# A DiT layer up to LayerNorm 1: the order of five engines read from a written list, the first two features in one group, warm-up matmuls only ahead of the first product

## The chip, the cores and the metric

The kernel runs on one core of a Trainium2 chip. It issues work to five engines: TensorE (PE in the profile, with its weight loads as PEld), VectorE (DVE), ScalarE (ACT), GpSimd (POOL) and SyncE (SP, which issues nearly all of the loads from device memory). Each engine takes its instructions strictly in the order in which they were issued to it. The metric is the device time of one execution, in microseconds (us). Lower is better.

## The reference

One layer of a diffusion transformer over 256 latent tokens `x` and 256 context tokens `ctx` with 2048 features, all in float32. Up to the place that matters here it computes:

```python
sh1, sc1, g1, sh2, sc2, g2 = silu(c) @ w_ada + b_ada          # split in six; w_ada is 2048 x 12288
csh1, csc1, ...            = silu(c_ctx) @ w_ada + b_ada
qa, ka, va, qb, kb, vb     = modulate(x, sh1, sc1) @ w_in     # modulate(x, s, c) = x * (1 + c) + s
qac, kac, vac, ...         = modulate(ctx, csh1, csc1) @ w_in
heads = concat(window_sink_attention(qa, ...), global_attention(qb, ...))
x = layer_norm(ALPHA * x + g1 * (heads @ w_out), ln1_g, ln1_b)
x = layer_norm(ALPHA * x + g2 * swiglu(modulate(x, sh2, sc2), ...), ln2_g, ln2_b)
```

So no product with `w_in` can start before a shift and a scale exist for its feature. Each shift and scale is a sum over a whole column of `w_ada`, 2048 rows long.

## The kernel before

**Tiles.** A "feature" below is a block of 128 of the 2048 model features, 0 to 15. A block of `w_in` has 512 output columns, and there are six, b = 0 to 5; blocks 2 and 5 hold keys and values and have four rows of outputs (two of `x`, two of `ctx`), the others hold queries and have two rows. A product in full float32 is three matmuls of 128x512 (`mm3`, L334 to 337): the weights are split into a rounded part `hi` and a remainder `lo`, and the scaled input into `uh` and `ul`. ACT makes `hi` (the cast in `flow_weights`, L603), DVE makes `lo` (L606).

**Groups.** `GROUPS` cuts the features into (0), (1), (2, 3), (4 to 7) and (8 to 15). For each group `flow_inputs` and `flow_columns` make a chain: load its columns of `w_ada`, sum them on PE into four partial rows (L654), copy these to SBUF on ACT (`ada`, L683), select and add on PE (L688), add the bias on DVE (`shc`, L694, and `scc`, L696); then transpose the inputs on PE ("flip", L822), scale them on ACT (`uf`, L828), cast on ACT (`uh`, L835), remainder on DVE (`ul`, L838). For features 12 to 15 (`VECTOR_K`) the columns are summed on DVE instead (`csum`, L716 and L718), transposed and reduced on DVE (L742, L745) and folded by PE (L769). `flow_block` then issues the products of one block with the group's features into an `acc` bank of PSUM. After a group, the result of a block goes to SBUF: for the first group as a copy (L887 on ACT, L891 on DVE), for the following ones as an addition on DVE (L889, into `qacc` or `kvacc`). From group number `SEED_G` = 3 on, the old sum is copied into the bank first, and no addition is needed.

**What sets the order.** Up to LayerNorm 1 nothing is issued directly. The functions named `flow_...` and some others add steps to an object `Flow`: engine, estimated time, the function that issues the instructions, the steps it comes after, and the buffers it takes and gives back. At build time `Flow.run` (L235) plans the order of all steps of all engines with a list scheduler forward and backward, tries 1400 random variations in a replay with estimated times, and issues the best. What comes after LayerNorm 1's scalars is issued by code behind `F.run()`.

**Warm-ups.** Besides five matmuls at the very start (`EARLY_WARM`), `WARM` = 56 further matmuls of `ident` with itself, whose result nobody reads, are steps of the plan (L1343). They have the lowest rank, each follows the one before, and together they hold one `wk` bank of PSUM until the last.

**First loads.** The ACT queue loads the first 128 columns of `x` and `ctx` (L380, L381). SP loads feature 0's columns of `w_ada`: 1 MB for the scale, 2 x 0.5 MB for the shift, 128 columns wide (rows of 512 bytes). Feature 1 follows with 2 MB of its own.

```python
for i in range(WARM):
    warms.append(F.add("PE", 430 if i < COLD else 225, lambda i=i: warm_step(i), [warms[-1]],
                       [wps] if i == 0 else [], [wps], at=1e6))
```

Of the kernel before, what the change touches and what calls it, by code (L numbers as in the profile page):

```python
# [23 lines left out]
P = 128  # L24
D = 2048
# [15 lines left out]
GROUPS = ((0, 1), (1, 1), (2, 2), (4, 4), (8, 8))  # L41
# [6 lines left out]
WARM = 56  # L48
VECTOR_K = (12,)
EARLY_WARM = 5  # L50
COLD = 3
SEED = 4
# [13 lines left out]
SEED_G = 3  # L66
# [3 lines left out]
GET_NS = 1300  # L70

# [11 lines left out]
class Flow:  # L83

    ENGINES = ("SP", "PE", "ACT", "DVE", "POOL")
    SAME = {"SP": 0, "PE": 0, "ACT": 120, "DVE": 80, "POOL": 80}
    OTHER = {"SP": 2000, "PE": 270, "ACT": 180, "DVE": 160, "POOL": 150}  # L90
    AGAIN = 1300
    ROUNDS = 8
    TRIES = 1400
    DRAWS = 4
    LATE = {"SP": 1000.0, "ACT": 100.0, "DVE": 100.0}

    def __init__(self, room, begin):
        self.room, self.begin, self.steps, self.at = dict(room), begin, [], 0.0

    def add(self, eng, ns, fn, after=(), take=(), give=(), at=None, since=0.0):  # L100
        s = Step()
        s.since = since
        s.eng, s.ns, s.fn, s.take, s.give = eng, ns, fn, take, give
        s.after = [a if isinstance(a, tuple) else (a, 0) for a in after if a is not None]
        s.rank = (self.at if at is None else at, len(self.steps))
        for b in give:
            b.left += 1
        self.steps.append(s)
        return s

    def lag(self, a, b):
        return (self.SAME if a.eng == b.eng else self.OTHER)[a.eng]

    def forward(self):

        room, free, back, order, now = dict(self.room), dict(self.begin), [], [], 0.0
        later, ready = ({e: [] for e in self.ENGINES} for _ in range(2))
        left = {b: b.left for s in self.steps for b in s.give}
        for s in self.steps:
            s.next, s.left, s.when = [], len(s.after), s.since  # L120
        for s in self.steps:
            for a, early in s.after:
                a.next.append((s, early))
            if not s.left:
                heapq.heappush(later[s.eng], (s.when, s.rank, s))
        while len(order) < len(self.steps):
            while back and back[0][0] <= now:
                room[heapq.heappop(back)[1]] += 1
            moved = False
            for e in self.ENGINES:  # L130
                while later[e] and later[e][0][0] <= now:
                    heapq.heappush(ready[e], heapq.heappop(later[e])[1:])
                if free[e] > now:
                    continue
                for item in sorted(ready[e]):
                    s = item[1]
                    pools = [next((p for p in b.pools if room[p] > 0), None) for b in s.take]
                    if None in pools or any(room[p] < pools.count(p) for p in pools):
                        continue
                    ready[e].remove(item)  # L140
                    heapq.heapify(ready[e])
                    for b, p in zip(s.take, pools):
                        b.pool = p
                        room[p] -= 1
                    s.start, free[e] = now, now + s.ns
                    for b in s.give:
                        left[b] -= 1
                        if left[b] == 0:
                            lag = self.AGAIN if b.loaded else self.OTHER[e]
                            heapq.heappush(back, (free[e] + lag, b.pool))  # L150
                    for n, early in s.next:
                        n.left -= 1
                        n.when = max(n.when, free[e] - early + self.lag(s, n))
                        if n.left == 0:
                            heapq.heappush(later[n.eng], (n.when, n.rank, n))
                    order.append(s)
                    moved = True
                    break
            if not moved:
                times = [free[e] for e in self.ENGINES if free[e] > now and (ready[e] or later[e])]  # L160
                times += [later[e][0][0] for e in self.ENGINES if later[e] and later[e][0][0] > now]
                times += [back[0][0]] if back else []
                if not times:
                    return None, None
                now = min(times)
        return order, max(s.start + s.ns for s in self.steps)

    def backward(self, end):

        free = {e: end for e in self.ENGINES}  # L170
        later, ready = ({e: [] for e in self.ENGINES} for _ in range(2))
        left, by, start, now = {s: len(s.next) for s in self.steps}, {s: end for s in self.steps}, {}, end
        for s in self.steps:
            if not left[s]:
                heapq.heappush(later[s.eng], (-end, -(s.start + s.ns), s.rank, s))
        while len(start) < len(self.steps):
            moved = False
            for e in self.ENGINES:
                while later[e] and -later[e][0][0] >= now:
                    heapq.heappush(ready[e], heapq.heappop(later[e])[1:])  # L180
                if free[e] < now or not ready[e]:
                    continue
                s = heapq.heappop(ready[e])[-1]
                start[s] = free[e] = now - s.ns
                moved = True
                for a, early in s.after:
                    left[a] -= 1
                    by[a] = min(by[a], start[s] + early - self.lag(a, s))
                    if left[a] == 0:
                        heapq.heappush(later[a.eng], (-by[a], -(a.start + a.ns), a.rank, a))  # L190
            if not moved:
                times = [free[e] for e in self.ENGINES if free[e] < now and (ready[e] or later[e])]
                now = max(times + [-later[e][0][0] for e in self.ENGINES if later[e] and -later[e][0][0] < now])
        return start

    def replay(self, order, draw):

        free, rooms, end, late = dict(self.begin), {p: [0.0] * n for p, n in self.room.items()}, {}, {}
        left = {b: b.left for s in self.steps for b in s.give}
        for s, pools in order:  # L200
            t = max(free[s.eng], s.since, *(end[a] - early + self.lag(a, s) for a, early in s.after), 0.0)
            for b, p in zip(s.take, pools):
                t = max(t, heapq.heappop(rooms[p]))
                b.pool = p
# [1768 lines left out]
```

## Time and profile before

| | |
|---|---|
| three runs | 1124.49, 1124.76, 1125.29 us (median 1124.76) |
| span of the profiled execution | 1124.1 us (the three runs are 0.4 to 1.2 us above it) |
| instructions | 14152 |
| warm-up matmuls of the plan (L1343) | 56, from 8.7 to 129.4 us |
| first product with `w_in` (L335) | 16.42 us |
| fold of the last column sums (L769) | 147.97 us |
| four flips that follow LayerNorm 1's scalars (L1510) | 393.79 us |

The profiler records two matmul passes for each float32 matmul of `ident`, of the sums (L654) and of the flips: "x30" of L1343 are 15 warm-ups. A matmul row's time begins when its data start to flow and ends at the modelled end, so rows overlap; the distance from one start to the next is what a matmul takes of PE's time. In the views by stage each line has the stretch, then busy time and count of PE, PEld, DVE, ACT and POOL, the granted clock of PE (1.00 is full), the busy share of the DMA engines and GB/s.

### The profile page before, as it was taken

How to read it: one execution, taken by the hardware profiler on the slowest of the kernel's cores; microseconds unless marked ns; L12 is line 12 of the kernel's file. 1: busy time of each engine (PE TensorE's matmuls, PEld its weight loads, DVE VectorE, ACT ScalarE, POOL GpSimd, SP SyncE). 2: the span in 40 equal slices, each digit the busy share in tenths (PEclk: the TensorE clock that was granted, in tenths of full speed). 3: DMA queues.
4: the chain of work that ended last, by engine and by line, in shares of the span. 5: the costliest groups of instructions: out<-in, count | busy, mean ns of one | idle time of the engine just before them, and what ended most of it. 6: DMA issues, size and time to landing. Idle time of an engine off the chain costs nothing.

```text
span 1124.1 us, 14152 instructions
## 1 busy us (share of the span) xinstructions
PE 1103.7 (98%) x5241; PEld 893.4 (79%) x5241; DVE 905.7 (81%) x1097; ACT 603.6 (54%) x879; POOL 47.1 (4%) x86
## 2 busy tenths in 40 slices
PE   8999999999999999999999999999999999999995
PEld 7677788788888778888888888888888788888884
DVE  3758999999989988787756876887875899678886
ACT  3335584787684355544464555655554565345541
POOL 1000050101200011000000000000000000000000
PEclk9999999999999999999999999999999999999998
DMA  9999999697999879989858798998896576546651
GB/s 298 388 391 373 390 366 370 225 312 215 356 311 375 303 284 341 326 309 340 295 189 297 264 340 273 314 308 302 311 321 222 159 253 223 190 149 231 225 217 75
DMA packets 179452, 321.27 MB, mean 286 GB/s; under 512 B 8979, under 2 KB 51379, under 8 KB 177077
## 3 DMA queue, kind: packets, MB, share of 16 engines
q1 hardware_dynamic: 177350, 319.23, 81.1%
q10 hardware_dynamic: 1808, 1.11, 0.3%
q8 instruction: 41, 0.67, 0.2%
q14 instruction: 29, 0.24, 0.1%
q0 software_dynamic: 224, 0.02, 0.0%
HBM read 304.07 MB, written 16.25 MB: 285 GB/s over the span
## 4 chain that ended last, share of the span: by engine, by line
PE 94%; DVE 3%; DMA 2%; issue 0%; ACT 0%; DVEq 0%; ACTq 0%
PE acc L335 22%; PE acc L336 22%; PE acc L337 22%; PE wk L337 7%; PE wk L336 7%; PE wk L335 7%; PE wk L1130 2%; PE wk L654 2%; PE wk L1343 1%; DMA raw<-in_w_in_dram 1%; PE wk L822 1%; DMA raw<-in_w_ada_dram 1%; DMA adav<-in_b_ada_dram 1%; DVE adav L454 0%; DVE lo L332 0%
## 5 line engine op out<-in xcount | busy, mean ns | idle before, releaser
L326 DVE TENSOR_TENSOR lo<-raw,hi 128x1024 fp32r<-128x1024 f32 x232 | 280.5, 1221 | 126.4 <-ACT hi L325 124.7
L325 ACT CAST hi<-raw 128x1024 fp32r<-128x1024 f32 x232 | 243.3, 1055 | 241.3 <-PE acc L337 130.7
L337 PE MATMUL acc<-hi,u2l 128*128 128x512 f32 x448 | 174.6, 390 | 1.4 <-DVE u2l L1686 1.4
L336 PE MATMUL acc<-lo,u2h 128*128 128x512 f32 x448 | 174.9, 390 | 0.0
L335 PE MATMUL acc<-hi,u2h 128*128 128x512 f32 x448 | 174.7, 391 | 0.0
L603 ACT CAST hi<-raw 128x1024 fp32r<-128x1024 f32 (+1 forms) x86 | 87.5, 1031 | 92.0 <-DMA raw<-in_w_in_dram 40.1
L454 DVE SCALAR_TENSOR_TENSOR adav<-raw,cs,adav 128x1024 f32<-128x1024 f32 (+1 forms) x96 | 114.3, 1191 | 6.1 <-DMA raw<-in_w_ada_dram 2.5
L606 DVE TENSOR_TENSOR lo<-raw,hi 128x1024 fp32r<-128x1024 f32 (+1 forms) x86 | 101.8, 1197 | 21.5 <-ACT hi L603 21.5
L335 PE MATMUL acc<-hi,uh 128*128 128x512 f32 x256 | 103.5, 404 | 0.2 <-DVE qacc L889 0.2
L335 PE MATMUL acc<-hi,hTh 128*128 128x512 f32 x264 | 102.7, 389 | 0.6 <-ACT hi L331 0.6
L336 PE MATMUL acc<-lo,hTh 128*128 128x512 f32 x264 | 102.7, 389 | 0.0
L337 PE MATMUL acc<-hi,hTl 128*128 128x512 f32 x264 | 102.5, 389 | 0.0
L337 PE MATMUL acc<-hi,ul 128*128 128x512 f32 x256 | 100.2, 391 | 0.0
L336 PE MATMUL acc<-lo,uh 128*128 128x512 f32 x256 | 99.9, 390 | 0.0
L337 PE MATMUL wk<-hi,u2l 128*128 128x512 f32 x256 | 99.6, 389 | 0.0
L336 PE MATMUL wk<-lo,u2h 128*128 128x512 f32 x256 | 99.6, 389 | 0.0
L335 PE MATMUL wk<-hi,u2h 128*128 128x512 f32 x256 | 99.6, 389 | 0.0
L337 PEld LDWEIGHTS acc<-hi,u2l 128*128 128x128 f32 x448 | 84.1, 188 | 19.3 <-DVE u2l L1686 2.0
L336 PEld LDWEIGHTS acc<-lo,u2h 128*128 128x128 f32 x448 | 84.1, 188 | 18.9 <-DVE lo L326 1.5
L335 PEld LDWEIGHTS acc<-hi,u2h 128*128 128x128 f32 x448 | 84.0, 188 | 18.3 <-ACT u2h L1685 1.0
L335 PEld LDWEIGHTS acc<-hi,uh 128*128 128x128 f32 x256 | 48.2, 188 | 16.1 <-issue 3.8
L335 PEld LDWEIGHTS acc<-hi,hTh 128*128 128x128 f32 x264 | 49.5, 188 | 11.3 <-ACT hi L331 1.0
(296 smaller groups left out, 1765.0 us busy)
## 6 DMA issues: line engine op xcount, KB each, us to landing
raw<-in_w_ada_dram SPq DMA_DIRECT2D x63, 1024.0 KB, 7.2
raw<-in_w_up_dram SPq DMA_DIRECT2D x44, 1024.0 KB, 6.7
raw<-in_w_gate_dram SPq DMA_DIRECT2D x44, 1024.0 KB, 6.5
raw<-in_w_down_dram SPq DMA_DIRECT2D x44, 1024.0 KB, 5.3
raw<-in_w_ada_dram SPq DMA_DIRECT2D x66, 512.0 KB, 6.3
raw<-in_w_in_dram SPq DMA_DIRECT2D x18, 1024.0 KB, 7.6
raw<-in_w_out_dram SPq DMA_DIRECT2D x16, 1024.0 KB, 7.6
pd<-hx SPq DMA_DIRECT2D x64, 128.0 KB, 3.7
```

The source lines that it names most:

```text
L325: nc.scalar.copy(hi[:, :n], raw[:, s : s + n])
L326: nc.vector.tensor_tensor(lo[:, :n], raw[:, s : s + n], hi[:, :n].bitcast(F32), op=ALU.subtract)
L335: nc.tensor.matmul(ps, lhsT=xh, rhs=w[0], start=first, stop=False, skip_group_check=seeded)
L336: nc.tensor.matmul(ps, lhsT=xh, rhs=w[1], start=False, stop=False, skip_group_check=seeded)
L337: nc.tensor.matmul(ps, lhsT=xl, rhs=w[0], start=False, stop=last, skip_group_check=seeded)
L454: nc.vector.scalar_tensor_tensor(a[:, c : c + piece], raw[:, f : f + piece], cs[:, 4 * (g * (G4 * NB // w) + j) + 2, None], a[:, c : c + p ...
L603: nc.scalar.copy(hl.hi[:, :n], raw.t[:, s : s + n])
L606: nc.vector.tensor_tensor(hl.lo[:, :n], raw.t[:, s : s + n], hl.hi[:, :n].bitcast(F32), op=ALU.subtract)
L654: nc.tensor.matmul(bank.t[32 * j : 32 * j + 32, :width], lhsT=cs[:, 4 * k + 2 - 2 * i : 4 * k + 34 - 2 * i], rhs=raw.t[:, c * width : (c + ...
L822: nc.tensor.transpose(ps.t[:, (j * 2 + t) * P : (j * 2 + t + 1) * P], src, ident)
L1130: nc.tensor.matmul(o_ps.t[:, : 2 * P].rearrange("p (g q) -> p g q", q=32), lhsT=v, rhs=pv[:, k], start=k == 0, stop=k == 3)
L1343: nc.tensor.matmul(wps, lhsT=ident, rhs=ident, start=True, stop=True)
```

## The change

The planner is gone. `Flow.run(order, warm)` takes a string `PLAN` of 1245 step numbers and issues the steps in that order, with `a` or `r` behind a number naming the pool that its buffer comes from; `wN` issues N warm-up matmuls at that place. The list holds `w6`, `w3`, `w7` and `w12`, all ahead of the first product: 28 in place of 56. They write a bank of the `acc` pool.

The first group is now features 0 and 1 together. Its columns of `w_ada` come in four loads of 1 MB, 256 columns wide (rows of 1 KB); the first loads of `x` and `ctx` are 256 columns wide. `SEED_G` goes from 3 to 2, so that the same features (4 to 7) are the first that are seeded. The branch of `flow_blocks` for groups of one feature is no longer reached. One group fewer means that each block's sum is evacuated and added to once less.

```diff
-GROUPS = ((0, 1), (1, 1), (2, 2), (4, 4), (8, 8))
+GROUPS = ((0, 2), (2, 2), (4, 4), (8, 8))
-WARM = 56
-COLD = 3
-SEED = 4
-SEED_G = 3
+SEED_G = 2
+PLAN = """
+4r 2r 1195 6a w6 3 5 0 w3 7 19 8a 946 w7 9 60r 10 1 61 14 11 1192 67r 49r 155a 27a 85r 13 12 15 16 17 20 50 68 21 22
+62 18 51 w12 63 64 69 52 56 86 38 23 65 66 87 70 55 74 72 76 37 89 59 28r 78r 79 80 31r 30r 116 137r 1193 73 77 29 71
...
+"""
-    def forward(self):
...
-    def run(self):
...
+    def run(self, order, warm):
+        left = {b: b.left for s in self.steps for b in s.give}
+        for word in order.split():
+            if word[0] == "w":
+                warm(int(word[1:]))
+                continue
+            s = self.steps[int(word.rstrip("abr"))]
...
+            s.fn()
...
-    first_cx = xt[:, :, D - P :]
-    nc.scalar.dma_start(xt[:, :, :P], x[:, :P].rearrange("(t p) d -> p t d", p=P))
+    first_cx = xt[:, :, D - 2 * P :]
+    nc.scalar.dma_start(xt[:, :, : 2 * P], x[:, : 2 * P].rearrange("(t p) d -> p t d", p=P))
...
+            if not c0 and not g:
+                for k in range(0, KD, nk):
+                    for i in range(2):
+                        r, ld = flow_load(w_ada, k, nk, i * D, width)
...
-                for i, k, m, since in ((0, 0, KD, 7200.0), (1, 0, KD // 2, 9700.0), (1, KD // 2, KD // 2, 11300.0)):
...
-    for i in range(WARM):
...
+            warm_room.append(acc_bank())
         for _ in range(n):
-            nc.tensor.matmul(wps, lhsT=ident, rhs=ident, start=True, stop=True)
+            nc.tensor.matmul(warm_room[0][:, :P], lhsT=ident, rhs=ident, start=True, stop=True)
...
-    T = 18.0
+    T = 9.0
...
-    F.run()
+    F.run(PLAN, warm)
```

Line numbers fall by 95 and more in the changed kernel: the products are L240 to 242, the column sums on PE L558, the selection L594, the copy `ada` L589, the flips L728, `lo` L510, the warm-ups L1253, DVE's column sums L622 and L624, the fold L675.

Three places show what the list moves.

**PE from its first column sums to the first product.** Before, `raw` is the 1 MB load of feature 0's scale, `raw_153` and `raw_156` the two halves of its shift:

```order
L654 MATMUL wk<-raw,cs 32x128 x16
L1343 MATMUL wk<-ident 128x128
L550 MATMUL wk<-ident,brow 128x96
L1343 MATMUL wk<-ident 128x128
L822 MATMUL wk<-ident,xt 128x128 x2
L654 MATMUL wk<-raw_153,cs 32x128 x8
L822 MATMUL wk<-ident,xt 128x128 x2
L1343 MATMUL wk<-ident 128x128 x2
L654 MATMUL wk<-raw_156,cs 32x128 x8
L1343 MATMUL wk<-ident 128x128 x3
L688 MATMUL wk<-sel,ada 128x4
L1343 MATMUL wk<-ident 128x128 x11
L335 MATMUL acc<-hi,uh 128x512
```

The same place in the changed kernel; the sums take the four loads of 1 MB, the first two in the one row of 16:

```order
L1253 MATMUL acc<-ident 128x128 x6
L558 MATMUL wk<-raw,cs 32x256 x16
L454 MATMUL wk<-ident,brow 128x96
L1253 MATMUL acc<-ident 128x128 x3
L558 MATMUL wk<-raw,cs 32x256 x8
L728 MATMUL wk<-ident,xt 128x128 x4
L1253 MATMUL acc<-ident 128x128 x7
L558 MATMUL wk<-raw,cs 32x256 x8
L728 MATMUL wk<-ident,xt 128x128 x4
L594 MATMUL wk<-sel,ada 128x4 x2
L1253 MATMUL acc<-ident 128x128 x12
L240 MATMUL acc<-hi,uh 128x512
```

Both features' sums, selections and flips stand ahead of the first product, and 28 warm-ups in place of 18.

**PE where features 4 to 7 get their shift and scale (80 us in the profile before).** Before, from the last product of features 0 to 3 to the first of features 4 to 7 (`uh_875`); the four rows of L688 are the selection, `wk_851` and `wk_870` flips of context tokens, `raw_781` and `raw_812` columns of the next group:

```order
L335 MATMUL acc_818<-hi_765,uh_599 128x512
L336 MATMUL acc_818<-lo_766,uh_599 128x512
L337 MATMUL acc_818<-hi_765,ul_600 128x512
L1343 MATMUL wk_177<-ident_70 128x128
L688 MATMUL wk_831<-sel_106,ada_779 128x4 x4
L1343 MATMUL wk_177<-ident_70 128x128 x5
L822 MATMUL wk_851<-ident_70,cxt_700 128x128 x4
L1343 MATMUL wk_177<-ident_70 128x128 x6
L822 MATMUL wk_870<-ident_70,cxt_700 128x128 x4
L654 MATMUL wk_878<-raw_781,cs_103 32x512 x4
L654 MATMUL wk_878<-raw_812,cs_103 32x512 x4
L335 MATMUL acc_825<-hi_802,uh_875 128x512
```

The selection (L594) of the same features in the changed kernel:

```order
L728 MATMUL wk_665<-ident_70,xt_76 128x128 x4
L728 MATMUL wk_670<-ident_70,cxt_356 128x128 x4
L728 MATMUL wk_675<-ident_70,cxt_356 128x128 x4
L594 MATMUL wk_682<-sel_106,ada_656 128x4 x4
L240 MATMUL acc_687<-hi_532,uh_250 128x512
L241 MATMUL acc_687<-lo_533,uh_250 128x512
L242 MATMUL acc_687<-hi_532,ul_251 128x512
L240 MATMUL acc_687<-hi_532,uh_250 128x512
L241 MATMUL acc_687<-lo_533,uh_250 128x512
L242 MATMUL acc_687<-hi_532,ul_251 128x512
L240 MATMUL acc_719<-hi_403,uh_507 128x512
```

The flips now stand ahead of the selection, and behind it 36 matmuls with the older features (`uh_250`, `uh_507` and others), one flip and eight sums come before the first one with features 4 to 7.

**DVE where the column sums of features 12 to 15 begin.** Before:

```order
L889 TENSOR_TENSOR qacc<-qacc,acc 128x512 x2
L694 TENSOR_TENSOR shc<-wk,bcol 128x8
L696 SCALAR_TENSOR_TENSOR scc<-wk,bcol 128x8
L838 TENSOR_TENSOR ul<-uf,uh 128x512 x2
L606 TENSOR_TENSOR lo<-raw,hi 128x1024
L838 TENSOR_TENSOR ul<-uf,uh 128x512 x2
L716 TENSOR_SCALAR csum<-raw,cs 128x1024 x2
L718 SCALAR_TENSOR_TENSOR csum<-raw,cs,csum 128x1024 x4
```

The changed kernel, where L795 is the addition, L797 the first group's copy and L600 and L602 the shift and scale:

```order
L795 TENSOR_TENSOR qacc<-qacc,acc 128x512
L797 COPY qacc<-acc 128x512
L622 TENSOR_SCALAR csum<-raw,cs 128x1024 x2
L624 SCALAR_TENSOR_TENSOR csum<-raw,cs,csum 128x1024
L600 TENSOR_TENSOR shc<-wk,bcol 128x8
L602 SCALAR_TENSOR_TENSOR scc<-wk,bcol 128x8
L510 TENSOR_TENSOR lo<-raw,hi 128x1024
L624 SCALAR_TENSOR_TENSOR csum<-raw,cs,csum 128x1024
L795 TENSOR_TENSOR qacc<-qacc,acc 128x512
L795 TENSOR_TENSOR kvacc<-kvacc,acc 128x512
```

The first column sums moved ahead of the shift and scale of features 4 to 7, among additions of the group before. Over the whole stretch up to the fold DVE has 16 additions in place of 32.

More of the change, by code (lines that the diff above doesn't have):

```diff
@@ L83, with __init__ @@
 class Flow:
[L88 to L98, printed above, removed]
+    def __init__(self, room):
+        self.room, self.steps, self.at = dict(room), [], 0.0
     def add(self, eng, ns, fn, after=(), take=(), give=(), at=None, since=0.0):
         s = Step()
[L102 to L105, printed above, removed]
+        s.eng, s.ns, s.fn, s.take, s.give, s.done = eng, ns, fn, take, give, False
+        s.after = [a[0] if isinstance(a, tuple) else a for a in after if a is not None]
         for b in give:
@@ L109, in add @@
         return s
-    def lag(self, a, b):
-        return (self.SAME if a.eng == b.eng else self.OTHER)[a.eng]
-    def forward(self):
-        room, free, back, order, now = dict(self.room), dict(self.begin), [], [], 0.0
-        later, ready = ({e: [] for e in self.ENGINES} for _ in range(2))
-        left = {b: b.left for s in self.steps for b in s.give}
[L119 to L204, printed above, removed]
-            free[s.eng] = t + s.ns
-            end[s] = free[s.eng] + draw.random() * (self.LATE.get(s.eng, 0.0) if s.ns else 0.0)
+    def run(self, order, warm):
+        left = {b: b.left for s in self.steps for b in s.give}
+        for word in order.split():
[3 more added lines that the diff above has]
+            s = self.steps[int(word.rstrip("abr"))]
+            assert not s.done and all(a.done for a in s.after)
+            for b in s.take:
+                b.pool = next((p for p in b.pools if len(b.pools) == 1 or p[0] == word[-1]))
+                self.room[b.pool] -= 1
+                assert self.room[b.pool] >= 0
+            s.fn()
+            s.done = True
@@ L258, in dit_layer @@
+                    self.room[b.pool] += 1
+        assert all(s.done for s in self.steps)
 @with_exitstack
@@ L539, in dit_layer @@
     fill(pa, 448)
-    F = Flow({"raw": RAW_BUFS, "araw": ADA_BUFS, "hl": HL_BUFS, "acc": 4, "wk": 4, "b4": NB4, "t2k": T2K},
-             {"SP": 1300.0, "PE": 7300.0, "ACT": 5000.0, "DVE": 4000.0, "POOL": 4000.0})
+    F = Flow({"raw": RAW_BUFS, "araw": ADA_BUFS, "hl": HL_BUFS, "acc": 4, "wk": 4, "b4": NB4, "t2k": T2K})
     pools = {"raw": wraw, "araw": araw}
@@ L1378, in dit_layer @@
         T += dur
-    start.after = [(last_load[0], 0)]
-    start.left = 1
+    start.after = [last_load[0]]
     gate_from = T
```

90 lines of the change are left out of this document (23 added, 67 removed), and 32 rows, old and new, of the table PLAN.

## The prediction

> **What bounds the kernel now.** I read the page's totals and its chain first, then PE's waits, then the warm-ups by themselves, and last PE's timeline around them.
>
> ```profile
> span 1124.1 us, 14152 instructions
> PE 1103.7 (98%) x5241; PEld 893.4 (79%) x5241; DVE 905.7 (81%) x1097; ACT 603.6 (54%) x879; POOL 47.1 (4%) x86
> PE 94%; DVE 3%; DMA 2%; issue 0%; ACT 0%; DVEq 0%; ACTq 0%
> ```
>
> PE sets the end: it is busy 98% of the span and holds 94% of the chain. Its waits beyond the start are few:
>
> ```profile
> PE acc L337 <- DVE u2l L1686: 1.4, 1, 1.4
> PE wk L654 <- DMA raw<-in_w_ada_dram: 1.1, 1, 1.1
> PE wk L688 <- ACT ada L683: 1.1, 1, 1.1
> PE wk L1510 <- DVE xt L1278: 0.5, 1, 0.5
> PE acc L335 <- DVE qacc L889: 0.2, 1, 0.2
> ```
>
> A busy share this high hides what the change is about: 56 of the matmuls are filler. From PE's timeline (start, duration; two recorded passes are one matmul):
>
> ```profile
> 13.97 2.70 PE L1343 MATMUL wk<-ident 128*128 128x128 f32 x22
> 16.42 0.48 PE L335 MATMUL acc<-hi,uh 128*128 128x512 f32 x1
> ...
> 28.38 1.95 PE L654 MATMUL wk<-raw,cs 128*32 128x128 f32 x64
> 30.27 0.94 PE L1343 MATMUL wk<-ident 128*128 128x128 f32 x6
> ...
> 32.27 0.39 PE L688 MATMUL wk<-sel,ada 128*128 128x4 f32 x2 [1.07 <-ACT ada L683]
> 32.51 0.41 PE L822 MATMUL wk<-ident,xt 128*128 128x128 f32 x2
> 32.76 0.38 PE L822 MATMUL wk<-ident,cxt 128*128 128x128 f32 x2
> 32.98 0.61 PE L1343 MATMUL wk<-ident 128*128 128x128 f32 x4
> 33.63 1.93 PE L654 MATMUL wk<-raw,cs 128*32 128x256 f32 x32
> ...
> 81.38 1.36 PE L1343 MATMUL wk<-ident 128*128 128x128 f32 x10
> 82.57 0.60 PE L822 MATMUL wk<-ident,cxt 128*128 128x128 f32 x4
> 83.01 1.50 PE L1343 MATMUL wk<-ident 128*128 128x128 f32 x12
> ...
> 126.16 3.51 PE L1343 MATMUL wk<-ident 128*128 128x128 f32 x30
> 147.97 0.26 PE L769 MATMUL wk<-cpart,fold 128*32 128x16 f32 x8
> ```
>
> Eleven warm-ups take 16.42 - 13.97 = 2.45 us, 0.223 each. The orders put 18 of the 56 ahead of the first product at 16.42 and 38 behind it: 8.47 us in which PE looks busy and waits. They sit where a feature group's chain is not ready (around 30 and 80) and where DVE is late (126). Whether these 8.5 us go is the whole question.
>
> **The change: the first product.** It will be later, for it needs both features.
>
> ```profile
> 29.00:32.00 3.00, 2.20 (x58) 1.81 (x46) 0.62 (x2) 1.51 (x3) 0.00 (x0) 1.00 1.10 361
> L835 ACT CAST uh<-uf 128x512 fp32r<-128x512 f32 x10 | 6.2, 629 | 0.1
> L838 DVE TENSOR_TENSOR ul<-uf,uh 128x512 fp32r<-128x512 f32 x8 | 5.4, 686 | 3.7 <-ACT uh L835 3.6
> 14.40 1.02 ACT L828 ACTIVATE uf<-wk,shc,scc 128x256 f32<-128x256 f32 x2 [0.95 <-DVE scc L696]
> L603 ACT CAST hi<-raw 128x1024 fp32r<-128x1024 f32 x26 | 26.8, 1051 | 33.4 <-DMA raw<-in_w_in_dram 31.7 <-PE acc L337 1.6
> ```
>
> Ahead of it now lie four loads of 1 MB (1.05 million bytes), 0.5 MB of inputs and the small rows, 4.8 million bytes. The row of 29 to 32 us, in which rows of 1 KB arrive, moves 361 GB/s: 13.3 us, and with a start near 2.2 us (from where the before trace shows loads, an estimate) the last lands near 16. Behind it on PE: eight sums (1.93/2, since the row at 33.63 is 16 of this size), four flips and two selections, some 0.9, with the copy by ACT between: about 18.2. Then ACT casts `hi` (1.05, ready near 19), scales two features (1.02), casts `uh` (0.63); the first matmul needs `uh`, near 20.7, and PE has 12 warm-ups (2.68) to end first, near 20.9. I take **21.3**, with 0.4 for hand-overs. Bounds: 20.5, if the loads run as in the denser stages, and 22.5, if PE's slow start (below) lasts as long as in this trace. That is 4.9 later than 16.42.
>
> **The change: from there to the fold.** Before, 147.97 - 16.42 = 131.55 us. What goes, in PE's time:
>
> - 38 warm-ups: 8.47.
> - Waits for feature 1's columns (1.1) and on an addition (0.2): 1.3. Feature 1 has no chain of its own any more.
> - Feature 1's sums (28.38 to 30.27), selection and flips (32.27 to 32.98): 2.6. They now lie ahead of the first product.
> - Twelve matmuls of products, which the order now has behind the fold. The rows L335 to L337 at 16.42 follow each other by 0.227: 2.72, given back later.
>
> That leaves 116.5. The wider loads cost PE nothing: 32 sums of 256 columns take what 64 of 128 did. The flips of features 4 to 7, before between two stretches of warm-ups, stand ahead of their selection, and 36 older products (36 x 0.227 = 8.2 us) stand behind it. The chain that this must cover is from selection to first use, 81.38 to about 84.5: 3 us. That cover is ample.
>
> **New waits.** The last stretch is where it can fail, since DVE and the loads are tight there.
>
> ```profile
> 55.00:97.00 42.00, 42.00 (x238) 30.16 (x238) 26.84 (x35) 19.14 (x30) 0.00 (x0) 1.00 1.04 391
> 97.00:148.00 51.00, 51.00 (x280) 38.51 (x279) 50.22 (x47) 29.64 (x46) 1.57 (x2) 1.00 1.01 366
> L889 DVE TENSOR_TENSOR qacc<-qacc,acc 128x512 f32<-128x512 f32 x16 | 10.8, 684 | 3.3 <-PE acc L337 3.3
> L889 DVE TENSOR_TENSOR kvacc<-kvacc,acc 128x512 f32<-128x512 f32 x16 | 10.6, 684 | 5.3 <-PE acc L337 5.1
> L606 DVE TENSOR_TENSOR lo<-raw,hi 128x1024 fp32r<-128x1024 f32 x26 | 31.7, 1234 | 9.4 <-ACT hi L603 9.4
> L606 DVE TENSOR_TENSOR lo<-raw,hi 128x512 fp32r<-128x512 f32 x4 | 2.8, 688 | 9.7 <-ACT hi L603 9.7
> L742 DVE STREAM_TRANSPOSE cturn<-csum 128x1024 f32<-128x1024 f32 x2 | 2.4, 1234 | 0.0
> L745 DVE TENSOR_REDUCE cpart<-cturn 128x32 f32<-128x1024 f32 x2 | 2.4, 1209 | 0.0
> 0.00:16.42 16.42, 5.42 (x36) 4.81 (x36) 1.00 0.95 283
> 16.42:130.00 113.58, 10.73 (x79) 9.61 (x77) 1.00 1.05 379
> ```
>
> Before, DVE is idle for 15 of the 42 us from 55 to 97 and then has no gap up to the fold (50.22 of 51). This is why 15 warm-ups stand at 126. The change takes 16 additions (16 x 0.684 = 10.9) and a net 1.5 of `lo` from it (four of 512 columns out, one of 1024 in), 12.4 in all, and starts the column sums earlier. DVE alone could then be done at 148.0 - 12.4 = 135.6. PE by the sum so far comes to the fold at 21.3 + 116.5 = 137.8. The loads: the `w_in` piece ahead of DVE's transposes ends 47.7 MB into the queues (sizes added up along the changed order); at the rates of the two windows above (283 GB/s for 16.42 us, then 379) that has landed at 130. A cast (1.05), two `lo` (2.47), two transposes (2.47) and two reductions (2.42) later it is 138.4. Three engines arrive within 3 us: I put **1.2** us of new waits in (the fold's 0.6, and as much for sums of the next group that stand close behind their load near 37 us). Bounds: 0, and 6, if the loads keep the 361 GB/s of the row at 29 in place of 379 (43.0 MB / 361 is 5.6 us more).
>
> **Costed at nothing.** The warm-ups held one of four `wk` banks up to 129 us; now they hold an `acc` bank, and only until the first product, when three others are free: nothing, or a little gain at the flips. The `ada` loads of features 12 to 15 begin in SP's queue behind 24.1 MB (before 29.9) and end behind 43.5 (before 44.1): the queue carries the same bytes, and what stands behind the moved loads, blocks of `w_in`, comes up to 6 MB later than before in mid-stage, some 15 us at 379 GB/s. The old products cover this, as DVE's and ACT's idle shares there show (26.84 and 19.14 of 42 us busy in the row of 55 to 97); without that cover it would be a part of the 6 us that bound the new waits. `bias` and `ones` on ACT, and `SEED_G`, change no work: the same features are seeded.
>
> **The rest.** From the fold to the end 1124.1 - 147.97 = 976.1, and 2.7 for the twelve matmuls moved there. The code behind LayerNorm 1 is the same. The two waits at its scalars (0.5 and 1.4 in the list above) depend on how much product is left behind the last load; I leave them, with bounds of 2 us off (both gone) and 2 us on (both doubled).
>
> **Sum:** 21.3 + 116.5 + 1.2 + 2.7 + 976.1 = 1117.8, 6.3 below the span of 1124.1. The profiled execution lies 0.66 under the median of 1124.76, so 1118.5. As a cross-check: 28 warm-ups fewer are 6.24 us, and the waits that come and go nearly cancel.
>
> **Rivals.**
>
> *The filled waits stay as bare ones (slower).* The warm-ups filled time in which nothing else could run; if the list can't put products there, since loads and DVE are no sooner, the 8.5 us are idle instead, and the later first product isn't made up for. 21.3 + 116.5 + 8.5 + 1.3 + 2.7 + 976.1 = 1126.4, about **1127**. It decides at the fold: with twelve matmuls behind it, break-even is a fold at 147.97 - 2.72 = 145.2. For it: the loads, which the change doesn't make smaller before the fold. Against: DVE's 12.4 us less, and the old products that now cover the chain at 80.
>
> *Only the long waits stay (no change).* The stretches at 81 to 84 (11 warm-ups, 2.45) and at 126 (15, 3.35) come back as idle time: 5.8 on, less the 1.2 counted: 1122.4, about **1123**.
>
> *A bare wait slows PE's clock behind it (also about no change).*
>
> ```profile
> 3.07 2.50 PE L384 MATMUL wk<-ident 128*128 128x128 f32 x10 [3.07 <-POOL ident masks.py:199]
> 6.88 1.94 PE L654 MATMUL wk<-raw,cs 128*32 128x128 f32 x32 [1.07 <-DMA raw<-in_w_ada_dram]
> 11.94 0.61 PE L1343 MATMUL wk<-ident 128*128 128x128 f32 x4
> ```
>
> The first five matmuls of `ident` take about 0.49 each, those at 13.97 take 0.223: PE starts at half pace and gets to full pace only near 12, some 5 us after work becomes steady at 6.88. Half of 5 us is lost, 2.5. If a wait as long as the 3.5 us at 126 puts PE back, it costs 3.5 + 2.5 in place of 1.2: about **1123**. The Trainium skill, TensorE: Matmul & The Clock Gate, Part 1: The HAM clock gate, states such a rule: after an idle window of about 3.4 us the array falls to half its clock, and needs about 3.4 us of sustained work to return. By that rule dropping the mid-stream warm-ups is a risk; the trace agrees at the start, and no run here yet shows a long wait later on.
>
> *All hand-overs fit (better).* No new waits, the first product at 20.5, the two late waits shorter: 1118.5 - 1.2 - 0.8 - 1.5 = **1115**.
>
> *The list does nothing but drop warm-ups that cost nothing* is excluded: they are on PE, which ends last.
>
> **How the numbers follow.** 0.2% (2.2 us) is what a measurement of this kernel can tell from no change. Forecast 0.65, better 0.13; both no-change rivals together 0.12; slower 0.10. Faster is thus 0.78. The forecast's own bounds, taken together where they are likely, are 1118.5 - 0.8 - 1.2 - 2.0 = 1114.5 and 1118.5 + 4.8 = 1123.3, the loads' bound. That includes both no-change rivals and leaves out the slower one and the tail of the better.
>
> **What would show it.** In the changed kernel's profile: 28 warm-ups (56 passes), none after about 21 us; the first product at 21.3 (not under 20.5 or over 22.5); the fold at 137.8 to 140, with DVE busy ahead of it and PE's waits before it under 6 us together; DVE's column sums from about 70 us on; the granted clock full in each stage after 20 us; the same 979 us from fold to end. A fold past 145 would make the prediction wrong, and so would a longer way from the fold to the end: then something in the list behind the fold counts that I took as unchanged.

## The result and the profile after

The changed kernel took 1118.17 us (median of 4 runs, 1117.67 to 1120.95), the kernel before 1125.03 beside it. The ratio is 0.9942, 95% interval 0.9928 to 0.9956: faster by 0.6%. The prediction was 1118.5. Over three batches, 14 runs of the changed kernel lie between 1116.96 and 1120.95, and a part of this spread is made in its first 25 us (below).

In the page's totals of the changed kernel, and in the list of PE's waits, the kernel is still PE's:

```profile
span 1115.9 us, 13859 instructions
PE 1095.1 (98%) x5121; PEld 886.5 (79%) x5121; DVE 895.3 (80%) x1075; ACT 602.6 (54%) x874; POOL 39.4 (4%) x86
PE wk L291 <- DMA crow<-in_c_ctx_dram: 3.0, 1, 3.0
PE wk L289 <- POOL ident masks.py:199: 2.2, 1, 2.2
PE wk L558 <- DMA raw<-in_w_ada_dram: 1.2, 1, 1.2
PE wk L594 <- ACT ada L589: 0.7, 1, 0.7
...
PE acc L242 <- DVE u2l L1579: 0.3, 1, 0.3
```

The first three are ahead of the first product. Behind it, up to the fold, a single wait of 0.7 us on the copy `ada` is left, at 130.69, where before 38 warm-ups filled 8.47 us. PE's timeline at the head, at the fold and at LayerNorm 1's flips (start, duration, line; two passes of a warm-up are one matmul):

```profile
7.97 2.93 PE L1253 MATMUL acc<-ident 128*128 128x128 f32 x12
12.07 1.93 PE L558 MATMUL wk<-raw,cs 128*32 128x256 f32 x32 [1.17 <-DMA raw<-in_w_ada_dram]
...
18.01 1.07 PE L558 MATMUL wk<-raw,cs 128*32 128x256 f32 x16
...
20.04 2.92 PE L1253 MATMUL acc<-ident 128*128 128x128 f32 x24
22.72 0.47 PE L240 MATMUL acc<-hi,uh 128*128 128x512 f32 x1
...
130.69 1.06 PE L594 MATMUL wk<-sel,ada 128*128 128x4 f32 x8 [0.70 <-ACT ada L589]
...
138.94 0.26 PE L675 MATMUL wk<-cpart,fold 128*32 128x16 f32 x8
...
387.61 0.60 PE L1403 MATMUL wk<-ident,xt 128*128 128x128 f32 x4
...
391.24 0.51 PE L242 MATMUL acc<-hi,u2l 128*128 128x512 f32 x1 [0.30 <-DVE u2l L1579]
```

No warm-up stands behind 22.7. The first product is 6.3 us later than before (22.72 against 16.42), the fold 9.0 us sooner (138.94 against 147.97). The four flips at 387.61 wait for nothing; before they waited 0.5, and the product behind them 1.4.

| stage, us | before | forecast | after |
|---|---|---|---|
| to the first product | 16.42 | 21.3 | 22.72 |
| first product to fold | 131.55 | 117.7 | 116.22 |
| fold to end of span | 976.1 | 978.8 | 976.96 |
| span | 1124.1 | 1117.8 | 1115.9 |
| run time less span | taken as 0.66 | 0.66 | 1.77 |

The last row is a correction. In all later runs, of this kernel and of the one before, the time is 1.7 to 1.9 us above the span of the same execution (1117.67 against 1115.9). So the profiled execution of before, with its span of 1124.1, was one of about 1125.9, some 1.1 us above the median. The prediction had taken the span's distance from the median of other runs for the overhead. The spans of the table fall by 8.2 us where the medians fall by 6.9: the profile of before is of an execution above its median, that of after is of the fastest of its four.

### The profile page after: what moved, and what is told of

It reads as the page before. It is cut to its first block, busy times and chain, and to the rows that moved or that the text cites. A ratio compares the mean times of both kernels' runs of the same rounds, so it can differ in the third digit from the quotient of the medians.

```text
span 1115.9 us, 13859 instructions
## 1 busy us (share of the span) xinstructions
PE 1095.1 (98%) x5121; PEld 886.5 (79%) x5121; DVE 895.3 (80%) x1075; ACT 602.6 (54%) x874; POOL 39.4 (4%) x86
## 4 chain that ended last, share of the span: by engine, by line
PE 93%; DVE 4%; DMA 2%; ACT 1%; issue 0%; SPq 0%; DVEq 0%; ACTq 0%
PE acc L240 22%; PE acc L242 22%; PE acc L241 22%; PE wk L242 7%; PE wk L241 7%; PE wk L240 7%; PE wk L1036 2%; PE wk L558 2%; DMA raw<-in_w_ada_dram 2%; DVE adav L359 1%; PE wk L728 1%; DMA adav<-in_b_ada_dram 1%; PE acc L1253 0%; DVE lo L237 0%; DVE m L986 0%
## 5 line engine op out<-in xcount | busy, mean ns | idle before, releaser
L231 DVE TENSOR_TENSOR lo<-raw,hi 128x1024 fp32r<-128x1024 f32 x232 | 281.1, 1222 | 126.7 <-ACT hi L230 124.8
L230 ACT CAST hi<-raw 128x1024 fp32r<-128x1024 f32 x232 | 243.8, 1055 | 242.3 <-PE acc L242 130.2
L240 PE MATMUL acc<-hi,u2h 128*128 128x512 f32 x448 | 175.4, 391 | 0.0
L507 ACT CAST hi<-raw 128x1024 fp32r<-128x1024 f32 x84 | 87.7, 1052 | 57.8 <-PE acc L242 36.8
L510 DVE TENSOR_TENSOR lo<-raw,hi 128x1024 fp32r<-128x1024 f32 x84 | 101.3, 1222 | 10.5 <-ACT hi L507 10.3
L240 PE MATMUL acc<-hi,hTh 128*128 128x512 f32 x264 | 102.8, 390 | 0.6 <-ACT hi L236 0.6
L240 PE MATMUL acc<-hi,uh 128*128 128x512 f32 x256 | 102.9, 402 | 0.0
L240 PE MATMUL wk<-hi,u2h 128*128 128x512 f32 x256 | 99.7, 390 | 0.0
L240 PEld LDWEIGHTS acc<-hi,u2h 128*128 128x128 f32 x448 | 84.2, 188 | 18.1 <-ACT u2h L1578 0.8
L240 PEld LDWEIGHTS acc<-hi,uh 128*128 128x128 f32 x256 | 48.2, 188 | 15.6 <-issue 2.1
L240 PEld LDWEIGHTS acc<-hi,hTh 128*128 128x128 f32 x264 | 49.6, 188 | 11.3 <-ACT hi L236 1.0
```

What stands on the lines that cost most here:

```text
L230: nc.scalar.copy(hi[:, :n], raw[:, s : s + n])
L231: nc.vector.tensor_tensor(lo[:, :n], raw[:, s : s + n], hi[:, :n].bitcast(F32), op=ALU.subtract)
L240: nc.tensor.matmul(ps, lhsT=xh, rhs=w[0], start=first, stop=False, skip_group_check=seeded)
L507: nc.scalar.copy(hl.hi[:, :n], raw.t[:, s : s + n])
L510: nc.vector.tensor_tensor(hl.lo[:, :n], raw.t[:, s : s + n], hl.hi[:, :n].bitcast(F32), op=ALU.subtract)
```

## The experiments

Four questions: were the mid-stream warm-ups cover or waste, is the gain the grouping's or the list's, is DVE a bound at the fold, and what sets the head and the late waits.

**1. The 38 late warm-ups left out of the kernel before.**

```diff
-        warm(wps.t, 1)
+        if i < 18:
+            warm(wps.t, 1)
```

> The kernel before with its plan, but only the 18 warm-ups ahead of the first product are issued; the 38 behind it (8.47 us of PE) are left out, and nothing else is moved. Filler theory (the warm-ups only filled waits that the planned order has anyway): 1124 to 1126 us, PE's idle time between 16 and 148 us up by about 8 us, fold still at 147 to 148.5 us. Clock theory (a bare wait of 3.4 us at 126 puts PE's clock back): 1126.5 to 1128, products behind that wait 0.45 us apart for some us. Waste theory (the warm-ups stood ahead of products that were ready): 1116 to 1119.

Measured: 1124.06 us, ratio 0.999 (0.998 to 1.0), so 1.1 us less than the 1125.14 beside it, just at the edge of what can be told from no change. By stage, in the view that gives a stretch, then busy time and count of PE, PEld, DVE, ACT and POOL, the granted clock, DMA share and GB/s:

```profile
0.00:17.52 17.52, 12.84 (x119) 10.83 (x119) 2.67 (x9) 4.82 (x11) 3.33 (x8) 1.00 0.97 286
17.52:146.08 128.56, 123.06 (x722) 86.84 (x721) 104.83 (x124) 64.54 (x102) 0.00 (x0) 1.00 1.04 377
97.00:146.08 49.08, 46.55 (x233) 32.97 (x232) 49.08 (x46) 28.44 (x45) 0.00 (x0) 1.00 1.00 368
```

From the first product (17.52 here) to the fold (146.08) PE is idle for 128.56 - 123.06 = 5.5 us: most of the 8.47 us of warm-ups comes back as waits, the longest 2.0, and DVE is busy for all of the 49 us ahead of the fold. The stretch is 3 us shorter, so about 3 us of it were waste; the fold, at 146.08, is sooner than the 147 to 148.5 expected, and the idle time is less than the 8 expected. The start takes back 1.1 (17.52 in place of 16.42), and 1.4 is lost behind the fold, which is 977.5 us from the end in place of 976.1: a wait of 1.5 us on `kTl` stands there that the profile of before doesn't have. The filler theory stands by the time: taking the warm-ups out is worth one microsecond; the rest of the change's gain had to come from making the waits go. In this profile the granted clock stayed full, so the clock theory did not act in it; the ten runs have mean clocks of 0.993 to 0.997, and the other runs were not profiled.

**2. The new grouping with the old planner.** Everything of the change but the list; 47 of the 56 warm-ups land ahead of the first product.

```diff
-GROUPS = ((0, 1), (1, 1), (2, 2), (4, 4), (8, 8))
+GROUPS = ((0, 2), (2, 2), (4, 4), (8, 8))
-SEED_G = 3
+SEED_G = 2
...
+                for k in range(0, KD, nk):
+                    for i in range(2):
+                        r, ld = flow_load(w_ada, k, nk, i * D, width)
...
```

> The changed grouping (features 0 and 1 together, four wide loads, SEED_G 2) with the planner of before and its 56 low-rank warm-ups; no written list. The planner puts 47 warm-ups ahead of the first product and 9 behind it. If the grouping alone (12.4 us less on DVE, no chain of feature 1's own) brings the gain: 1117 to 1120 us. If the list brings it: 1123 to 1126. I expect a first product near 24.3, 1.6 later than with the list, and in between: 1120 to 1122.

Measured: 1133.04 us, ratio 1.0069 (1.0054 to 1.0084): slower than before, which no theory had. The profile is of the slowest of its four runs (1133.91):

```profile
26.32 1.15 ACT L837 CAST uh<-uf 128x512 fp32r<-128x512 f32 x2
27.00 0.49 PE L335 MATMUL acc<-hi,uh 128*128 128x512 f32 x1
...
144.20 0.26 PE L771 MATMUL wk<-cpart,fold 128*32 128x16 f32 x8
399.45 1.09 PE L1507 MATMUL wk<-ident,xt 128*128 128x128 f32 x4 [5.02 <-DVE xt L1280]
400.19 0.78 PE L335 MATMUL acc<-hi,u2h 128*128 128x512 f32 x1
395.00:400.00 5.00, 0.55 (x3) 0.58 (x4) 3.50 (x7) 0.00 (x0) 0.00 (x0) 0.82 0.72 277
400.00:405.00 5.00, 5.00 (x18) 4.36 (x17) 0.37 (x2) 2.81 (x7) 0.27 (x1) 0.50 0.64 210
405.00:410.00 5.00, 5.00 (x16) 3.87 (x15) 4.75 (x10) 1.68 (x3) 1.67 (x3) 0.65 0.01 1
410.00:415.00 5.00, 5.00 (x24) 4.13 (x23) 3.93 (x5) 3.77 (x5) 0.00 (x0) 1.00 0.24 36
```

The fold comes at 144.2, 3.8 us sooner than before, where the list's comes 9.0 sooner. The difference lies in the head: the first product is at 27.00, where 24.3 was expected and the list's is at 22.72. There are 19 more warm-ups ahead of it (4.2 us), and ACT casts `uh` only at 26.32; which of the two makes it late was not separated. From the first product to the fold it takes 117.2 us, against 116.22 with the list and 131.55 before. So in that stretch nearly all of the gain comes with the grouping, without the list. At LayerNorm 1, behind everything that was regrouped, PE stands bare for 5.0 us. Then the granted clock is 0.50 until about 408 us, and a product of 0.39 us takes 0.63. Against the list's kernel the lag grows there from 6.6 us (390.02 against 383.38, the first product behind LayerNorm 1) to 15.5, and is 15.8 at the last product. What the list brings beyond the grouping is the sooner start and the way past LayerNorm 1.

**3. The same with that wait filled.** To tell the wait from the work behind it:

```diff
         ps = wk_bank()
+        for _ in range(22 if t and not kk else 0):
+            nc.tensor.matmul(ps[:, :P], lhsT=ident, rhs=ident, start=True, stop=True)
```

> The changed grouping with the planner, and 22 more warm-ups put ahead of the second tile's flips behind LayerNorm 1, where PE stood bare for 5.0 us and then ran at half pace until 408 us. They add 4.9 us of PE work. Clock theory (the bare wait, not the work behind it, cost 9 us): 4 to 4.6 us less than without them, 1128 to 1129.5, granted clock 1.00 from 395 to 410. Rival (the clock falls for another reason, or the wait costs only its own length): no gain, 1132.5 to 1134 or more.

Measured: 1130.99 us (ratio 1.005, 1.0036 to 1.0065), 2.05 less than without the 22 matmuls. The two intervals overlap, and the total lies outside the 1128 to 1129.5 expected.

```profile
200.00:205.00 5.00, 3.01 (x12) 2.27 (x11) 4.99 (x9) 2.12 (x6) 0.00 (x0) 0.79 0.64 219
205.00:210.00 5.00, 5.00 (x24) 3.78 (x23) 3.80 (x6) 3.38 (x15) 0.00 (x0) 0.87 0.52 162
395.00:400.00 5.00, 5.00 (x38) 4.65 (x37) 0.99 (x5) 0.00 (x0) 0.00 (x0) 1.00 1.03 376
400.00:405.00 5.00, 4.37 (x34) 3.91 (x33) 4.70 (x9) 1.86 (x5) 0.00 (x0) 1.00 0.48 156
405.00:410.00 5.00, 4.73 (x23) 3.69 (x23) 4.96 (x12) 3.11 (x7) 2.17 (x3) 1.00 0.53 195
```

The clock stays at 1.00 through 395 to 410, and the way from the first product behind LayerNorm 1 to the end (392.67 here, 390.02 there, to the ends of the spans at 1131.3 and 1132.1) is 738.7 us in place of 742.1: 3.4 us won by adding 4.9 us of PE work. The expected 4 to 4.6 was too much for the total, since in this profile another bare wait, of 2.0 us on `kTl` up to 202.82, is followed by half clock at 200 to 210, where the kernel of experiment 2 waits 1.2 us and has no such stretch. Why it waited longer there was not followed. This profile is of the slowest of the four runs (1133.11, mean clock 0.994); the two runs with 0.996 took 1129.48 and 1130.13.

**4. DVE's saved additions put back.**

```diff
                 elif g > 0:
                     nc.vector.tensor_add(dst, dst, ps.t)
+                    nc.vector.tensor_tensor(dst, dst, dst, op=ALU.max)
```

> The changed kernel with one more DVE operation of 0.69 us behind each of the 16 additions ahead of the fold (an elementwise maximum of the sum with itself; the values stay). 11 us come back to DVE. Theory that DVE arrives at the fold together with PE, so that the additions saved count: DVE has 5.4 us of idle time at 52 to 83 us to absorb them, the fold comes 4 to 5.5 us later, 1122 to 1124 us, with a wait of PE at or near the fold. Rival that PE alone sets the pace and DVE's work is covered: 1118 to 1119.

Measured: 1124.29 us (ratio to before 0.9988, 0.9978 to 0.9997), 6.1 above the changed kernel's 1118.17 of the other batch and 5.7 above the median of all its 14 runs.

```profile
55.00:97.00 42.00, 39.28 (x209) 26.05 (x208) 37.20 (x53) 17.74 (x27) 0.00 (x0) 1.00 1.00 374
97.00:146.82 49.82, 48.58 (x239) 36.01 (x238) 49.64 (x45) 29.05 (x49) 0.00 (x0) 0.97 0.98 368
135.00:140.00 5.00, 3.76 (x26) 3.11 (x23) 5.00 (x8) 4.54 (x8) 0.00 (x0) 0.88 1.04 392
140.00:145.00 5.00, 5.00 (x20) 4.13 (x20) 5.00 (x6) 4.97 (x10) 0.00 (x0) 0.78 1.04 408
146.82 0.26 PE L675 MATMUL wk<-cpart,fold 128*32 128x16 f32 x8
```

The first product stands at 24.27 in this profile, so from there to the fold it is 122.55 us, 6.3 longer than with the change. DVE has no gap ahead of the fold any more (49.64 of 49.82), and PE idles for 1.24 us there, after 2.72 us from 55 to 97. 1.2 + 2.2 us of the stretch from 135 to 145 ran at half pace (0.12 x 5 x 2 and 0.22 x 5 x 2), which costs 1.7. Of the remaining 4.6, 3.3 are waits more than with the change (1.24 + 2.72, less the 0.7), most of them well ahead of the fold, and 1.3 is not attributed. Without the half clock the 4.6 would be within the 4 to 5.5 expected, although DVE had more idle time to absorb the work than was taken: 9.9 us from 52 to 83 in the changed kernel's profile, not 5.4. DVE's work ahead of the fold counts for a large part of the gain: with 11 us of it back, little is left.

**5. Warm-ups ahead of the fold in the changed kernel.**

```diff
             ps.t = wk_bank()
+            for _ in range(8):
+                nc.tensor.matmul(ps.t[:, :P], lhsT=ident, rhs=ident, start=True, stop=True)
             fold_parts(ps.t, part, 2 * ncol)
```

> The changed kernel with 8 warm-ups put just ahead of the fold (1.78 us of PE, written into the bank that the fold then overwrites). Theory that PE has no spare time left there, so that a warm-up costs its full length now: 1.5 to 2.0 us more than the changed kernel of this job. Rival that DVE or the loads are the ones waited for: under 0.6 more.

Measured: 1120.71 us (ratio to before 0.9961, 0.9948 to 0.9975) against 1118.56 of the changed kernel in this batch: 2.15 more, a little over the range.

```profile
140.03 1.95 PE L659 MATMUL wk<-ident 128*128 128x128 f32 x16
141.90 0.26 PE L677 MATMUL wk<-cpart,fold 128*32 128x16 f32 x8
```

In the profile the first product is at 23.89 and the fold at 141.90: 118.0 us, 1.8 more than 116.2, just what eight matmuls take. PE has no spare time left at the place where the planned order had 15 warm-ups.

**6. The head.** The list's sums began with the second load, though the first lands earlier, and 10 warm-ups stood between the later sums.

```diff
-4r 2r 1195 6a w6 3 5 0 w3 7 19 8a 946 w7 9 60r
+2r 4r 1195 6a w6 3 5 0 7 19 8a 946 9 60r
```

> The changed kernel with the 3 and 7 warm-ups between the sums taken out (18 left: 6 and 12), and the first two loads in the order in which their sums are made. Theory that PE's own queue (sums that start only with the second load at 12.1, then 10 warm-ups) sets the first product, not the fourth load (landed at 17.1): first product 0.7 to 1.0 us sooner, 21.7 to 22.0, and 1117.2 to 1117.6 us. Rival that the loads or ACT's chain set it: 22.5 to 22.8, time unchanged. Rival that fewer warm-ups leave PE at half pace: first product later than 22.8 or products up to 25 us 0.45 apart, 1119 or more.

Measured: 1117.25 us, 1116.22 to 1117.46 (ratio 0.9928, 0.9913 to 0.9943).

```profile
10.77 2.09 PE L558 MATMUL wk<-raw,cs 128*32 128x256 f32 x32
...
16.56 1.07 PE L558 MATMUL wk<-raw,cs 128*32 128x256 f32 x16 [1.05 <-DMA raw<-in_w_ada_dram]
...
21.27 0.48 PE L240 MATMUL acc<-hi,uh 128*128 128x512 f32 x1
...
38.64 1.94 PE L558 MATMUL wk<-raw,cs 128*32 128x256 f32 x32 [0.99 <-DMA raw<-in_w_ada_dram]
...
138.59 0.26 PE L675 MATMUL wk<-cpart,fold 128*32 128x16 f32 x8
```

Now PE waits for the last load (1.05 us), and the first product is 1.45 us sooner, more than the 0.7 to 1.0 expected. The last load is summed at 16.56, as soon as it has landed; in the changed kernel it had landed at 17.1 and was summed at 18.01. So about 0.9 of the 1.45 is PE's own queue, and the rest a load that landed sooner. The two edits were made together and not told apart.

Little of it lasts: at 38.64 PE then waits 0.99 us for a load of the next group, for which the changed kernel had not to wait, and the fold is only 0.35 us sooner (138.59 against 138.94). The time, 0.9 below the 1118.17 of the other batch, is within the 1117.2 to 1117.6 expected, but the changed kernel was not run beside it in this batch.

**7. The changed kernel again, and two more heads.** In several profiles the sums at the head took twice as long, so the changed kernel was run again (twice), once with its head filled (the first diff), and once with the short head and four warm-ups between the first sums (the second):

```diff
-4r 2r 1195 6a w6 3 5 0 w3 7 19 8a 946 w7 9 60r
+4r 2r 1195 6a w10 3 5 0 w3 7 19 8a 946 w7 9 60r
```

```diff
-4r 2r 1195 6a w6 3 5 0 w3 7 19 8a 946 w7 9 60r
+2r 4r 1195 6a w6 3 w4 5 0 7 19 8a 946 9 60r
```

> The changed kernel itself, beside the others of this job, so that differences of one microsecond can be read: 1117.5 to 1119 us.

> As the short head (loads in the order of their sums, no warm-ups between the later sums), but 4 warm-ups stand between the first load's sums and the second's, where PE was bare for up to 2.3 us and in one profile stayed at half pace until 16 us. 22 warm-ups in all. Theory that the head is set by the fourth load and that this gap alone makes the clock come late: first product at 21.0 to 21.7 in every execution, median 1116.6 to 1117.5, 0.7 to 1.5 below the changed kernel of this job, spread of the runs under 1.5 us. Rival that the loads land 1 to 2 us apart from run to run anyway: same median as the changed kernel within 0.5, same spread.

> The changed kernel once more, as the measure for this job. If its executions come in two kinds by the clock in the head, they are near 1117.7 and near 1119.9, with nothing between 1118.6 and 1119.3.

> The changed kernel with 10 in place of 6 warm-ups ahead of the first column sums, and no other edit: PE has no bare time while the second load is on its way (0.9 to 2.3 us in the profiles). Theory that this bare time decides whether PE is still at half pace for the sums: all five executions near the lower of the two kinds, 1117.4 to 1118.4 us, first product 22.4 to 23. Rival that the two kinds come from the loads or from later places: two kinds as before, median within 0.5 us of the changed kernel of this job.

| kernel | median, us | runs |
|---|---|---|
| changed (batch of the short filled head) | 1119.80 | 1117.71 to 1120.26 |
| short head, filled | 1117.61 | 1117.16 to 1120.41 |
| changed (batch of the filled head) | 1118.56 | 1116.96 to 1120.47 |
| head filled | 1118.82 | 1117.99 to 1119.08 |

From the third profile of the changed kernel, of a run of 1120.47, and then from the one of the filled head:

```profile
7.89 2.93 PE L1253 MATMUL acc<-ident 128*128 128x128 f32 x12
11.68 3.64 PE L558 MATMUL wk<-raw,cs 128*32 128x256 f32 x32 [0.85 <-DMA raw<-in_w_ada_dram]
...
25.05 0.47 PE L240 MATMUL acc<-hi,uh 128*128 128x512 f32 x1
```

```profile
7.79 4.16 PE L1253 MATMUL acc<-ident 128*128 128x128 f32 x20
11.89 1.93 PE L558 MATMUL wk<-raw,cs 128*32 128x256 f32 x32
```

The same 16 sums take 3.64 us in one execution and 1.93 in another, after the same warm-ups and a similar gap; the first product is then at 25.05 in place of 22.72. That explains the upper end of the spread. Six profiles have this head, and the records of the granted clock in their traces, which no view lists, tell when it first became full. In the three of the changed kernel this was at 11.11, 11.57 and 17.50 us, with first products at 22.72, 22.45 and 25.05; in those of experiments 5, 4 and 8 it was at 14.88, 15.93 and 16.23, with first products at 23.89, 24.27 and 24.45. So first products of this head differ by up to 2.6 us without any edit to it.

The forecast of two kinds is kept in its letter: of all 14 runs of the changed kernel eight lie between 1116.96 and 1118.57, six between 1119.61 and 1120.95, and none between. The theory that the bare gap ahead of the sums decides is not shown: the clock was full soonest behind a gap of 1.17 us and latest behind one of 0.85. With the gap filled the spread of five runs is 1.1 us in place of 3.5, but the median is not lower (1118.82, above the 1117.4 to 1118.4 expected), and with the short filled head, where four warm-ups fill the wait for the second load, one of five runs still took 1120.41, a spread of 3.25 us where under 1.5 was expected. What decides it stays open.

The short filled head is 2.2 us below the changed kernel of its batch (ratio to before 0.9934, 0.9921 to 0.9947, against 0.995, 0.9936 to 0.9964). The intervals overlap; over all batches the nine runs of the two short heads have a median of 1117.33, the 14 of the changed kernel one of 1118.6. That a short head is faster is likely, and not shown.

**8. Three steps at LayerNorm 1.**

```diff
-1183 1221 1222 1184 1185 1165 1189 1190 1223 1224a 1230r 1243 1225 1244 1226a
+1183 1184 1185 1165 1189 1190 1224a 1230r 1243 1221 1222 1223 1225 1244 1226a
```

> The changed kernel with one pair of steps put back where the planned order had them: the fold of the second shift's columns (16 matmuls, 1.84 us of PE) and its copy on DVE go behind the last product of w_out and the first flips, in place of 4.5 us ahead. Theory that this place made the two late waits (on the scaled tile and on u2l) shrink from 2.0 to 0.3 us: 1.2 to 1.8 us more than the changed kernel of this job, both waits back. Rival that the order of DVE's additions did it: within 0.4 us.

Measured: 1124.79 us (ratio to before 0.9997, 0.9987 to 1.0008), 5.0 above the changed kernel of its batch. From PE's list of waits:

```profile
PE wk L1403 <- DVE xt L1184: 2.0, 1, 2.0
PE acc L240 <- ACT u2h L1578: 1.5, 1, 1.5
```

The three are 16 matmuls (1221), the copies of their result on DVE (1222) and three small operations on GpSimd (1223) that need the copies. Their place does decide the late waits, but the price was put far too low: 3.5 us of waits come back, more than the 2.0 that before had, and the second is now on `u2h` and not on `u2l`. There is no drop of the clock around them in this profile. From the fold to the end of the span it is 981.0 us, 4.0 more than with the change. The first product of this profile, at 24.45, is 2.0 later than in the changed kernel's profile of the batch (22.45); its clock was full only at 16.23. Its ten runs spread from 1122.84 to 1126.91, and those above 1126 have a mean clock of 0.992 to 0.993, where the lower ones have 0.994 to 0.996: in some executions the waits seem to put the clock back too. No profile of such a run was taken. Three of 1245 steps give back nearly the whole gain.

## Why the prediction was right, step by step

- **The mechanism.** 28 warm-ups fewer, and the waits that they filled gone too, as forecast. Experiment 1 shows that the first without the second is worth 1.1 us. Experiment 4 shows that the waits come back when DVE has its work back, experiment 5 that PE has no spare time left at the fold. Experiment 2 shows that from the first product to the fold the grouping with the old planner is within 1 us of the change: there what the grouping brings counts (less work on DVE, no chain of feature 1's own), and the list's order counts in the head and at LayerNorm 1. No wait came back at 80 or at 126, which rules out the rival that the long waits stay.
- **The first product, 21.3 forecast, 22.72 measured,** and up to 25.05 in another profile. This is outside the bounds (20.5 to 22.5). The step let the last load land near 16, with the rate of a later window, and the 12 warm-ups begin at 18.2. The load landed at 17.1, its sums started at 18.01 and the warm-ups at 20.04. It had the right order of work on PE behind that; experiment 6 shows the two things overlooked: sums that begin with the second load, and warm-ups that had become part of the path, 0.9 us together. PE's slow start was in the bound, but at too small a size: a clock that is full only at 17.50 in place of 11.11 goes with a first product 2.3 us later.
- **From there to the fold, 117.7 with 1.2 of new waits; 116.22 measured, with 0.7.** The 0.7 is neither of the two waits that were put in: it is on ACT's copy `ada`, 8 us ahead of the fold, while neither the fold nor the sums of the next group have a wait. The sums were close to one: with a first product 1.45 us sooner they wait 0.99 us, at 38.64 where 37 was put (experiment 6). Most of the other 1 us is a term that was too small. In the two timelines the times from each product's start to the next start add up to 94.18 us for 396 products before and 90.32 for 384 after. That is 3.86 less, where 2.72 and a wait of 0.2 were put in. A product behind another kind of matmul takes about 0.33 us and not 0.227, as the one at 16.42 does before (the next starts at 16.74), and there are 28 such places now in place of 35, which is 0.7 of it.
- **DVE, PE and loads within 3 us at the fold.** DVE is busy for 41.01 of the last 42 us and its last reduction ends at 138.79, where the fold begins. PE waits for no load in this stretch (below, the stage, the reductions in DVE's timeline, and DVE's additions as groups):

```profile
97.00:139.00 42.00, 41.30 (x221) 30.58 (x216) 41.01 (x38) 25.07 (x41) 0.00 (x0) 1.00 1.04 393
136.49 2.30 DVE L651 TENSOR_REDUCE cpart<-cturn 128x32 f32<-128x1024 f32 x2
L795 DVE TENSOR_TENSOR qacc<-qacc,acc 128x512 f32<-128x512 f32 x8 | 5.5, 682 | 1.2 <-PE acc L242 1.2
L795 DVE TENSOR_TENSOR kvacc<-kvacc,acc 128x512 f32<-128x512 f32 x8 | 5.4, 682 | 5.8 <-PE acc L242 5.7
```

- **The rest, 978.8 forecast, 976.96 measured.** The two late waits, left as they were in the sum, shrank from 2.0 to 0.3 us. The prediction had this as a lower bound. Experiment 8 shows which steps it hangs on.
- **The overhead.** 0.66 was 1.77. The span was forecast 1.9 us too long and the overhead 1.1 too small, so the closeness of 1118.5 to 1118.17 is partly luck; the drop itself was forecast as 6.3 and measured as 1125.03 - 1118.17 = 6.9. Within it a first product 1.4 us too late was made up for by a way to the fold that was 1.5 shorter than forecast; that, too, is luck.
- **The rivals.** "Filled waits stay bare" is what experiment 1 does with the old order and grouping; the changed kernel avoids it. "A bare wait slows the clock" does not happen in the changed kernel's three profiles behind the head, but experiments 2 and 3 show it, and its price was put too low: in experiment 2 a wait of 5.0 us cost 8.9 (the lag's growth from 6.6 to 15.5), 3.9 beyond its own length where 2.5 was put. The Trainium skill's rule (TensorE: Matmul & The Clock Gate, Part 1: The HAM clock gate) that idle time halves PE's clock agrees with that trace, where the clock is at half from 398.24 on and PE's wait ends at 399.45; its figure of about 3.4 us of work to return does not: there it was 9 us, up to 408.48.

## What to carry to other kernels

A filler instruction on the bounding engine says that something is waited for; removing the filler gained 1.1 of 8.5 us here as long as the waits behind it stayed, and the place to look is the engine that has no gap in that stage (here DVE ahead of the fold). A regrouping that saves work can lose time at a place that it doesn't touch, so read the lag of a later stage before judging it. Compare a profiled execution's span only with that execution's own time.

## What the runs showed of the hardware that was not expected

- **A bare wait of 1.99 us was followed by half clock** in experiment 3 (the row at 200), while one of 2.02 us in experiment 1 and one of 1.96 us in experiment 8 were not: the length alone doesn't decide.
- **The half-pace stretches have steps.** At 200 to 210 and at 135 to 145 they add up to 3.4 us (0.21 x 10 + 0.13 x 10, and 0.12 x 10 + 0.22 x 10), at 395 to 410 to 10.3 us (0.18 x 10 + 0.50 x 10 + 0.35 x 10), about three times as much. The clock records of these traces give the stretches themselves: 3.413 us at 202.92 (experiment 3) and at 138.80 (experiment 4), and 10.240 us, three times 3.413, at 398.24 (experiment 2). The full stretches between are multiples as well: 385.706 us is 113 times 3.413, and 122.880 is 36 times.
- **In the head the granted clock reads 1.00 while the matmuls run at half pace.** The stretch that holds the 3.64 us row, in the same profile:

```profile
10.00:16.00 6.00, 5.14 (x40) 2.89 (x40) 0.00 (x0) 0.00 (x0) 0.00 (x0) 1.00 1.09 386
```

There the distance between starts tells the pace, and the clock column does not: the clock record of this trace begins with the first full stretch, at 17.50, and the column shows what lies ahead of the record as full.
